# The MLP's first product by seven block products per pair of groups, with the sums of its weights held in place

## The chip, the cores and the metric

The kernel runs on one core of a Trainium2 chip. The metric is the time of one execution on the device in microseconds (us); the kernel before was run three times. A difference of about 0.2% (some 2 us) is what such a measurement can tell from none.

## What is computed

A decoder trunk of two layers on 512 tokens of 1024 features, all in 32-bit floats: a gated linear attention and an MLP, then a stick-breaking attention and an MLP, each followed by a layer norm. The change touches the MLPs, and to a small part the output product of the first attention:

```python
def sq_relu_mlp(x, w_up, w_down):
    h = jax.nn.relu(x @ w_up)       # (512, 1024) @ (1024, 4096)
    return (h * h) @ w_down         # (512, 4096) @ (4096, 1024)

h = layer_norm(DEEPNORM_ALPHA * h + sq_relu_mlp(h, mlp_w_up[layer], mlp_w_down[layer]),
               ln_g[layer, 1], ln_b[layer, 1])
```

## The kernel before

Every matrix is split into a high part that TensorE's fast 32-bit type holds exactly and a low part that is the rest: ScalarE (ACT) writes the high part (line 70 for weights, 98 for token matrices), VectorE (DVE) subtracts it from the whole (lines 72 and 99). A product is then three matmuls: high by high, high by low, low by high. Weights come from device memory in tiles of 128 partitions by 1024 (512 KB); their high and low parts live in pools of six tiles each (`split_tile`), so a split can run at most three pairs of tiles ahead of the product that uses it.

The MLP of a layer has eight groups of 512 of the 4096 inner features. `up(g)` makes one group of the squared first product: 96 matmuls of 512 columns, weights as the stationary side (lines 93 to 95), then relu on ACT (701) and a multiplication on DVE (703) into a tile `s2`. Only group 0 runs in halves of 256 columns. `down(g)` takes a pair of groups and adds its share of the second product to the rows `h`. It calls `seven`, which does the 2 by 2 blocks of that product by seven block products instead of eight, with sums of blocks of the tokens (lines 288, 360, 362, 374) and of the weights: 168 matmuls of 512 columns (line 346) in place of 192. In what follows the products of a `seven` are counted first to seventh in the order of the code. Each token block is split by `split_a` (lines 98 and 99).

Two of the four weight blocks are sums from the start: the tile is loaded by SyncE's queue (line 311) and a second block is added to it by an accumulating transfer that GpSimd (POOL) issues (line 305). The other two sums are made on DVE (lines 370 and 380), except in a call with `ends`, which adds blocks of device memory by more such transfers. The weight blocks live in eight tiles tagged B; a tile of the next call can be loaded only when its place is free.

The order of work in a layer's MLP:

```python
        sq = [up(0), up(1)]
        for h in hs:
            h.affine(vec, tc.keep_in_program_order)
        for g in range(0, NG - 2, 2):
            sq.append(up(g + 2))
            for _ in down(g):
                pass
            if g < NG - 4:
                sq.append(up(g + 3))
```

So an `up` lies ahead of each `down` whose group that `down` doesn't need yet, and the last `down` follows `up(7)` at once. The order of instructions on each engine is made by a scheduler when the program is built, unless a line says `keep_in_program_order`; on the chip each engine takes its queue in that order.

## Time and profile before

| | |
|---|---|
| median of three runs | 1120.47 us (1119.93 to 1120.68) |
| the profiled execution | 1120.0 us, of which the span from first to last instruction is 1118.1 us |
| TensorE clock granted | 0.999 of full |
| TensorE busy | 1110.2 us (99% of the span) |
| VectorE, ScalarE, GpSimd busy | 804.6, 551.2 and 166.2 us |
| transfers | 157.52 MB, 141 GB/s over the span |

Rows of a timeline give start and duration in us; a matmul's duration covers its way through the array, and the next one starts before it ends, so what a matmul costs in a stream is the distance between starts. "PEld" is the load of a matmul's stationary side.

### The profile page before, as it was taken

How to read it: one execution, taken by the hardware profiler on the slowest of the kernel's cores; microseconds unless marked ns; L12 is line 12 of the kernel's file. 1: busy time of each engine (PE TensorE's matmuls, PEld its weight loads, DVE VectorE, ACT ScalarE, POOL GpSimd, SP SyncE). 2: the span in 40 equal slices, each digit the busy share in tenths (PEclk: the TensorE clock that was granted, in tenths of full speed). 3: DMA queues.
4: the chain of work that ended last, by engine and by line, in shares of the span. 5: the costliest groups of instructions: out<-in, count | busy, mean ns of one | idle time of the engine just before them, and what ended most of it. 6: DMA issues, size and time to landing. Idle time of an engine off the chain costs nothing.

```text
span 1118.1 us, 14356 instructions
## 1 busy us (share of the span) xinstructions
PE 1110.2 (99%) x5519; PEld 920.1 (82%) x5519; DVE 804.6 (72%) x981; ACT 551.2 (49%) x829; POOL 166.2 (15%) x199
## 2 busy tenths in 40 slices
PE   9999999999999999999999999999999999999998
PEld 7888888898888888888888777778988888888886
DVE  4688649948956856858945888887489767667677
ACT  4455437643533534535634666664445435336363
POOL 1011222110100100122100434330200000000221
PEclk9999999999999999999999999999999999999999
DMA  8441399493670770887344121211946816706784
GB/s 250 120 132 57 112 261 221 132 256 113 189 207 24 200 208 19 204 199 143 113 114 132 57 76 39 76 38 56 276 122 191 245 52 164 231 19 186 178 131 89
DMA packets 105368, 157.52 MB, mean 141 GB/s; under 512 B 12306, under 2 KB 37266, under 8 KB 105300
## 3 DMA queue, kind: packets, MB, share of 16 engines
q1 hardware_dynamic: 87060, 120.96, 33.6%
q0 software_dynamic: 18240, 35.66, 18.6%
q8 instruction: 43, 0.70, 0.3%
q14 instruction: 25, 0.20, 0.1%
HBM read 153.45 MB, written 3.15 MB: 140 GB/s over the span
## 4 chain that ended last, share of the span: by engine, by line
PE 97%; DVE 2%; issue 0%; POOL 0%; POOLq 0%; DVEq 0%
PE ps L346 30%; PE ps L93 20%; PE ps L94 20%; PE ps L95 20%; PE ps L845 2%; PE ps L831 2%; PE ps L794 2%; PE ps L228 1%; PE ps L566 0%; DVE lo L72 0%; PE ps L121 0%; PE ps L631 0%; DVE bst L175 0%; PE ps L442 0%; PE ps L459 0%
## 5 line engine op out<-in xcount | busy, mean ns | idle before, releaser
L346 PE MATMUL ps<-hi,T 128*128 128x512 f32 x1008 | 313.2, 390 | 0.0
L93 PE MATMUL ps<-T,hi 128*128 128x512 f32 (+1 forms) x768 | 288.5, 376 | 0.0
L94 PE MATMUL ps<-T,hi 128*128 128x512 f32 (+1 forms) x768 | 285.5, 372 | 0.0
L95 PE MATMUL ps<-T,lo 128*128 128x512 f32 (+1 forms) x768 | 285.4, 372 | 0.0
L72 DVE TENSOR_TENSOR lo<-raw,hi 128x1024 fp32r<-128x1024 f32 x134 | 162.9, 1219 | 133.3 <-ACT hi L70 132.8
L70 ACT ACTIVATE hi<-raw 128x1024 fp32r<-128x1024 f32 x134 | 142.1, 1064 | 179.4 <-PE ps L94 61.3
L346 PEld LDWEIGHTS ps<-hi,T 128*128 128x128 f32 x1008 | 189.0, 188 | 40.0 <-DVE T L99 1.0
L346 PE MATMUL ps<-lo,T 128*128 128x512 f32 x504 | 196.1, 389 | 0.0
L70 ACT ACTIVATE hi<-B 128x1024 fp32r<-128x1024 f32 x108 | 114.1, 1059 | 160.4 <-PE ps L94 102.0
L72 DVE TENSOR_TENSOR lo<-B,hi 128x1024 fp32r<-128x1024 f32 x108 | 130.8, 1220 | 84.7 <-ACT hi L70 84.7
L95 PEld LDWEIGHTS ps<-T,lo 128*128 128x128 f32 x768 | 144.7, 188 | 25.1
L93 PEld LDWEIGHTS ps<-T,hi 128*128 128x128 f32 x768 | 144.7, 188 | 24.6 <-issue 0.9
L94 PEld LDWEIGHTS ps<-T,hi 128*128 128x128 f32 x768 | 144.8, 189 | 23.8 <-DVE T L99 0.2
L305 POOL DMA_DIRECT2D B<-in_mlp_w_down_dram x52 | 62.4, 1228 | 539.3 <-DMA B<-in_mlp_w_down_dram 424.7
L346 PEld LDWEIGHTS ps<-lo,T 128*128 128x128 f32 x504 | 94.6, 188 | 19.5
L93 PE MATMUL ps<-hi,T 128*128 128x512 f32 x256 | 102.4, 400 | 0.0
L95 PE MATMUL ps<-hi,T 128*128 128x512 f32 x256 | 100.1, 391 | 0.0
L94 PE MATMUL ps<-lo,T 128*128 128x512 f32 x256 | 100.0, 391 | 0.0
L168 DVE TENSOR_TENSOR h<-h,ps 128x512 f32<-128x512 f32 x110 | 74.7, 681 | 7.3 <-PE ps L95 4.2
L822 POOL TENSOR_TENSOR w<-w,r 128x512 f32<-128x512 f32 x32 | 53.0, 1658 | 131.6 <-DVE r L821 123.8
L821 DVE TENSOR_TENSOR_SCAN r<-r,begin 128x512 f32<-128x512 f32 x40 | 66.2, 1659 | 2.4 <-ACT r L818 2.2
L95 PEld LDWEIGHTS ps<-hi,T 128*128 128x128 f32 x256 | 48.1, 188 | 10.5 <-DVE T L99 0.2
(179 smaller groups left out, 1158.3 us busy)
## 6 DMA issues: line engine op xcount, KB each, us to landing
raw<-in_mlp_w_up_dram SPq DMA_DIRECT2D x64, 512.0 KB, 4.6
B<-in_mlp_w_down_dram SPq DMA_DIRECT2D x64, 512.0 KB, 6.0
B<-in_mlp_w_down_dram POOLq DMA_DIRECT2D x52, 512.0 KB, 7.9
raw<-in_gla_w_in_dram SPq DMA_DIRECT2D x20, 512.0 KB, 3.7
raw<-in_mlp_w_down_dram SPq DMA_DIRECT2D x16, 512.0 KB, 4.7
raw<-in_kv_w_dram SPq DMA_DIRECT2D x16, 512.0 KB, 4.2
B<-in_gla_w_o_dram POOLq DMA_DIRECT2D x14, 512.0 KB, 8.0
B<-in_gla_w_o_dram SPq DMA_DIRECT2D x8, 512.0 KB, 7.0
```

Of the source, the lines that this page charges most:

```text
L70: nc.scalar.activation(hi, raw, AF.Copy)
L72: nc.vector.tensor_tensor(lo, raw, hi.bitcast(F32), op=ALU.subtract)
L93: nc.tensor.matmul(ps, lhsT=a[0], rhs=b[0], start=first, stop=False)
L94: nc.tensor.matmul(ps, lhsT=a[0], rhs=b[1], start=False, stop=False)
L95: nc.tensor.matmul(ps, lhsT=a[1], rhs=b[0], start=False, stop=last)
L168: nc.vector.tensor_tensor(h, h, ps, op=op)
L305: nc.gpsimd.dma_start(out=b.rearrange("p (a b) -> p a b", a=2), in_=weights(k, h, j), accum_op=ALU.add)
L346: nc.tensor.matmul(banks[s], lhsT=a(k, s)[x], rhs=b[k][y], start=opens and (k, x, y) == (0, 0, 0), stop=closes and (k, x, y) == (3, 1, 0), ...
L794: nc.tensor.matmul(zs[b + a][:, at], lhsT=self.q[x][own, P * i:P * i + P], rhs=self.k[y][own, 0:n], start=(x + y == 0), stop=(x == 1), ski ...
L821: nc.vector.tensor_tensor_scan(down, down, begins[kind][:, ::-1], 1.0, op0=ALU.mult, op1=ALU.max)
L822: (nc.vector if kind == 2 else nc.gpsimd).tensor_tensor(w, w, r[:, 1:S + 1], op=ALU.mult)
L831: nc.tensor.transpose(out=ps[:, P * b:P * b + P], in_=w[:, P * b:P * b + P], identity=ident)
```

## The change

Groups 2 to 7 are no longer made by `up`, but in pairs by a new `up_seven(g, tokens)`: 2 by 2 blocks (two halves of the 1024 features, two halves of the 512 tokens, two groups), seven block products of 48 matmuls each. A moving side is a block of 256 tokens, so these matmuls are 256 columns wide and there are 336 to a pair, where two `up` had 192 of 512. The loop becomes: `down(g)`, then `up_seven(g + 2)`, whose two outputs the next `down` takes. No other product lies between them. The sums of token blocks are made once for a layer by `token_sums` after the first `down`, on DVE.

A new class `Blocks` loads the weight blocks for both kinds of call. It loads the two plain blocks first, then the two that are sums. The third and fourth sums (`third_sum`, `fourth_sum`) are now kept in program order on DVE behind the additions of results that stand before them in the code; with `ends` they are transfers from one B tile to another on the chip, not from device memory. Token sums in `seven` overwrite their inputs. The pools of high and low weight parts go from six tiles to five, the token tiles from eight to ten; the layer norm's vectors are loaded into tiles of other pools. In `up`, all even columns' squares go to ACT.

```diff
-        hi = wts.tile([P, 1024], F32R, tag="hi", bufs=6, name=nm("hi"))
+        hi = wts.tile([P, 1024], F32R, tag="hi", bufs=5, name=nm("hi"))
-    def ahead(a1, seventh=True):
-
-        s1, s2 = (lambda u: (u[:, :, 0:256], u[:, :, 256:512]))(unit(F32))
+    def ahead(a1):
+
         first = split_a(a1[:, :, 0:256])
-        nc.vector.tensor_tensor(s2, a1[:, :, 0:256], a1[:, :, 256:512], op=ALU.subtract)
-        return s1, s2, first, split_a(s2) if seventh else None
+        less = quarter()
+        nc.vector.tensor_tensor(less, a1[:, :, 0:256], a1[:, :, 256:512], op=ALU.subtract)
+        return first, lambda: split_a(less)
+    class Blocks:
+        def __init__(self, weights, pool):
+            self.weights, self.bs = weights, [[None] * 4 for _ in range(2)]
+            for i, k, j, other in ((2, 0, 0, None), (3, 1, 0, None), (1, 0, 1, (0, 0)), (0, 1, 1, (0, 1))):
+                for four_b, h in zip(self.bs, range(2)):
+                    b = pool.tile([P, 1024], F32, tag="B", bufs=8, name=nm("B"))
+                    nc.sync.dma_start(out=b.rearrange("p (a b) -> p a b", a=2), in_=weights(k, h, j))
+                    if other:
+                        self.more(b, h, *other)
+                    four_b[i] = b
+        def third_sum(self, ends):
+            for h, (b22, b12, b11, b21) in enumerate(self.bs):
+                if ends:
+                    nc.gpsimd.dma_start(out=b11, in_=b22, accum_op=ALU.add)
+                else:
+                    tc.keep_in_program_order(nc.vector.tensor_tensor(b11, b22, b11, op=ALU.add))
+        def fourth_sum(self, ends):
+            for h, (b22, b12, b11, b21) in enumerate(self.bs):
+                if ends:
+                    nc.gpsimd.dma_start(out=b21, in_=b11, accum_op=ALU.add)
+                else:
+                    tc.keep_in_program_order(nc.vector.tensor_tensor(b21, b21, b11, op=ALU.add))
...
-        tt(s1, a22, a21, op=ALU.subtract)
-        third = split_a(s1), split_b(1)
-        minus(s2, s1, a11)
+        seventh = seventh()
+        tt(a21, a22, a21, op=ALU.subtract)
+        third = split_a(a21), split_b(1)
+        minus(a11, a21, a11)
         product(*second, xs, True, True, 0, 0, last=True)
-        fourth = split_a(s2), split_b(2)
+        w.third_sum(ends)
+        fourth = split_a(a11), split_b(2)
         product(*third, zs, True, False, 1, 1)
-        minus(a12, a12, s2)
+        minus(a12, a12, a11)
         product(*fourth, ys, False, False, 0, 1)
+        w.fourth_sum(ends)
...
+        def up_seven(g, tokens):
+            w = Blocks(lambda k, h, j: block(mlp_w_up[l], 512 * k + 256 * h, 512 * (g + j)), mlp_)
...
+            def part(s, a, b, banks, opens, closes):
+                for f in (2 * s, 2 * s + 1):
+                    at = banks[s][:, 256 * (f % 2):256 * (f % 2) + 256]
+                    for k in range(4):
+                        for x, y in ((0, 0), (0, 1), (1, 0)):
+                            nc.tensor.matmul(at, lhsT=b[k][x][:, 128 * f:128 * f + 128], rhs=a(k)[y],
...
+            def close(s, banks, i, j, whole=False):
+                o = place(s, i, j)
+                if not whole:
+                    nc.vector.tensor_tensor(o, o, flat(banks[s]), op=ALU.add)
+                nc.scalar.activation(o, flat(banks[s]) if whole else o, AF.Relu, scale=-1.0 if j else 1.0)
+                nc.scalar.activation(o, o, AF.Square)
...
+            product(first, w.split(2), ys, True, False, keep, 0, 0)
+            product(second, w.split(3), xs, True, True, close, 0, 0)
+            w.third_sum(False)
+            product(third, w.split(1), zs, True, False, keep, 1, 1)
+            product(fourth, w.split(2), ys, False, False, keep, 0, 1)
+            product(third_, w.plain(1, 1), zs, False, True, close, 0, 1)
+            w.fourth_sum(False)
+            product(seventh, w.split(0), ys, False, False, close, 1, 1)
+            product(fourth_, w.split(3), ys, False, True, close, 1, 0, True)
+            return out
-        sq = [up(0), up(1)]
-        for h in hs:
-            h.affine(vec, tc.keep_in_program_order)
+        sq = [up(0), up(1, complete)]
         for g in range(0, NG - 2, 2):
-            sq.append(up(g + 2))
             for _ in down(g):
                 pass
-            if g < NG - 4:
-                sq.append(up(g + 3))
-        last, begun = up(NG - 1, lambda: ahead(sq[NG - 2]))
-        sq.append(last)
-        steps = down(NG - 2, begun=begun, norms=range(NT) if l == 0 else (2, 3), ends=True)
-        got = done(steps, work)
+            if g == 0:
+                tokens = token_sums()
+            sq = up_seven(g + 2, tokens)
+        steps = down(NG - 2, norms=range(NT) if l == 0 else (2, 3), ends=True)
+        got = done(steps, work, mlp_)
```

The scheduler's order moves in three places. First, on DVE before, layer 0, in the `up(3)` that runs ahead of `down(2)` (s_ is a group's tile, T_ a token tile, B_ a weight block, lo_ a low part; after "<-" stand the inputs):

```order
L703 TENSOR_TENSOR s_3040<-ps_2943,s_3040 128x512
L370 TENSOR_TENSOR B_3198<-B_3192,B_3198 128x1024
L362 TENSOR_TENSOR T_3202<-s_3040,s_2609 128x4x256
L99 TENSOR_TENSOR T_3246<-s_3040,T_3246 128x4x256
L360 SCALAR_TENSOR_TENSOR T_3202<-T_3202,s_2609 128x4x256
L72 TENSOR_TENSOR lo_3251<-B_3190,hi_3249 128x1024
L360 SCALAR_TENSOR_TENSOR s_3040<-s_3040,T_3202 128x4x256
L380 TENSOR_TENSOR B_3190<-B_3190,B_3188 128x1024
L72 TENSOR_TENSOR lo_3255<-B_3200,hi_3253 128x1024
L380 TENSOR_TENSOR B_3200<-B_3200,B_3198 128x1024
```

These are sums for `down(2)`: of its tokens (362, 360) and of its weights (370, 380). In the changed kernel the same sums of `down(4)` stand on DVE in the down itself. From its start (s_3574 and s_3575 are the two outputs of `up_seven(4)`; h_ rows are additions of finished products):

```order
L72 TENSOR_TENSOR lo_4091<-B_4018,hi_4089 128x1024
L290 TENSOR_TENSOR raw_4033<-s_3574 128x1024
L166 TENSOR_TENSOR h_1641<-h_1641,ps_4043 128x512
L385 TENSOR_TENSOR s_3574<-s_3575,s_3574 128x4x256
L166 TENSOR_TENSOR h_1642<-h_1642,ps_4057 128x512
L99 TENSOR_TENSOR T_4082<-raw_4033,T_4082 128x4x256
L99 TENSOR_TENSOR T_4086<-s_3574,T_4086 128x4x256
L72 TENSOR_TENSOR lo_4095<-B_4021,hi_4093 128x1024
L339 SCALAR_TENSOR_TENSOR s_3574<-s_3574 128x4x256
L166 TENSOR_TENSOR h_1641<-h_1641,ps_4098 128x512
L166 TENSOR_TENSOR h_1642<-h_1642,ps_4112 128x512
L316 TENSOR_TENSOR B_4010<-B_4024,B_4010 128x1024
```

and, six rows further, until the low part of the fifth product's tokens (T_4196):

```order
L166 TENSOR_TENSOR h_1644<-h_1644,ps_4153 128x512
L339 SCALAR_TENSOR_TENSOR s_3575<-s_3575,s_3574 128x4x256
L166 TENSOR_TENSOR h_1641<-h_1641,ps_4043 128x512
L72 TENSOR_TENSOR lo_4203<-raw_4199,hi_4201 128x1024
L166 TENSOR_TENSOR h_1642<-h_1642,ps_4057 128x512
L323 TENSOR_TENSOR B_4014<-B_4014,B_4010 128x1024
L323 TENSOR_TENSOR B_4016<-B_4016,B_4012 128x1024
L99 TENSOR_TENSOR T_4196<-s_3575,T_4196 128x4x256
```

The token and weight sums have moved from the `up` before into the `down`. Between these two fences stand the second third sum, T_4128, lo_4133, lo_4137 and the addition of ps_4139: from lo_4091 to T_4196 it is 25 rows.

Second, on DVE at the seam of the first `down` and the first `up_seven` of layer 0 (T_2776 is the room of the token sums, raw_2786 a part of one; the lo_ of B_2800 and B_2802 serve the first product, B_2811 the third):

```order
L164 SCALAR_TENSOR_TENSOR h_1644<-h_1644,ps_2525 128x512
L99 TENSOR_TENSOR T_2779<-T_2776,T_2779 128x4x256
L741 TENSOR_TENSOR T_2776<-T_2776,raw_2786 128x4x256
L72 TENSOR_TENSOR lo_2824<-B_2800,hi_2822 128x1024
L72 TENSOR_TENSOR lo_2828<-B_2802,hi_2826 128x1024
L99 TENSOR_TENSOR T_2777<-T_2776,T_2777 128x4x256
L72 TENSOR_TENSOR lo_2884<-B_2804,hi_2882 128x1024
L339 SCALAR_TENSOR_TENSOR T_2776<-T_2776,T_1653 128x4x256
L72 TENSOR_TENSOR lo_2888<-B_2806,hi_2886 128x1024
L748 TENSOR_TENSOR T_2776<-T_2776,T_1654 128x4x256
L72 TENSOR_TENSOR lo_2950<-B_2808,hi_2948 128x1024
L339 SCALAR_TENSOR_TENSOR T_2776<-T_2776,T_1655 128x4x256
```

Before, no row of this kind stood there: the splits of an `up` followed the additions of a `down` directly. Four rows further down (a split, a sum and an addition among them) stands lo_2954 of B_2811.

Third, on SyncE's queue, the loads of `down(4)` in the changed kernel, with the loads of `up_seven(4)` ahead of them and of `up_seven(6)` behind:

```order
L301 DMA B_3568<-in_mlp_w_up_dram 128x2x512
L301 DMA B_3571<-in_mlp_w_up_dram 128x2x512
L301 DMA B_4010<-in_mlp_w_down_dram 128x2x512
L301 DMA B_4012<-in_mlp_w_down_dram 128x2x512
L301 DMA B_4014<-in_mlp_w_down_dram 128x2x512
L301 DMA B_4016<-in_mlp_w_down_dram 128x2x512
L301 DMA B_4018<-in_mlp_w_down_dram 128x2x512
L301 DMA B_4021<-in_mlp_w_down_dram 128x2x512
L301 DMA B_4024<-in_mlp_w_down_dram 128x2x512
L301 DMA B_4027<-in_mlp_w_down_dram 128x2x512
L64 DMA raw_4199<-in_mlp_w_down_dram 128x2x512
```

and before, the loads of `down(2)`, between them those of an `up` (raw_):

```order
L311 DMA B_3182<-in_mlp_w_down_dram 128x2x512
L311 DMA B_3185<-in_mlp_w_down_dram 128x2x512
L311 DMA B_3188<-in_mlp_w_down_dram 128x2x512
L311 DMA B_3190<-in_mlp_w_down_dram 128x2x512
L64 DMA raw_2922<-in_mlp_w_up_dram 128x2x512
L64 DMA raw_2928<-in_mlp_w_up_dram 128x2x512
L311 DMA B_3192<-in_mlp_w_down_dram 128x2x512
```

The eight B tiles now pass from one call straight to the next: B_4018 and B_4021 take the place of the two tiles that the fourth sum of `up_seven(4)` reads last.

More of the change, by code (lines that the diff above doesn't have):

```diff
@@ L300, in seven @@
         a11, a21, a12, a22 = a1[:, :, lo_t], a1[:, :, hi_t], a2[:, :, lo_t], a2[:, :, hi_t]
[L301 to L329 removed]
+        w = Blocks(weights, pool)
+        split_b, plain_b = w.split, w.plain
         seen = set()
@@ L353, in product @@
                 add(s, banks, i, j, last)
-        s1, s2, first, seventh = begun or ahead(a1)
+        first, seventh = begun or ahead(a1)
         product(first, split_b(2), ys, True, False, 0, 0)
@@ L654, in yoco_kernel @@
     gate(1, 1, pcs)
-    begun = ahead(onT[0], seventh=False)
+    begun = ahead(onT[0])
     turn_gated(0, 1)
@@ new lines, in up_seven, with place, flat, keep @@
+        def up_seven(g, tokens):
+            w = Blocks(lambda k, h, j: block(mlp_w_up[l], 512 * k + 256 * h, 512 * (g + j)), mlp_)
+            first, second, third, fourth, third_, seventh, fourth_ = tokens
+            out = [four(), four()]
+            ys, xs, zs = ([None, None] for _ in range(3))
+            def part(s, a, b, banks, opens, closes):
+                if opens:
+                    banks[s] = bank()
+                for f in (2 * s, 2 * s + 1):
[3 more added lines that the diff above has]
+                            nc.tensor.matmul(at, lhsT=b[k][x][:, 128 * f:128 * f + 128], rhs=a(k)[y],
+                                             start=opens and (f % 2, k, x, y) == (0, 0, 0, 0),
+                                             stop=closes and (f % 2, k, x, y) == (1, 3, 1, 0),
+                                             skip_group_check=True)
+            def place(s, i, j):
+                return out[j][:, 2 * s:2 * s + 2, 256 * i:256 * i + 256]
+            def flat(ps):
+                return ps.rearrange("p (a b) -> p a b", a=2)
+            def keep(s, banks, i, j):
+                nc.scalar.activation(place(s, i, j), flat(banks[s]), AF.Copy)
+            def close(s, banks, i, j, whole=False):
[4 more added lines that the diff above has]
+                nc.scalar.activation(o, o, AF.Square)
+            def product(a, b, banks, opens, closes, then, *args):
+                for s in range(2):
+                    part(s, a, b, banks, opens, closes)
+                    then(s, banks, *args)
+            product(first, w.split(2), ys, True, False, keep, 0, 0)
[8 more added lines that the diff above has]
+            return out
@@ L857, in yoco_kernel @@
     parts = [(oA.hi[0][:, i, :], oA.lo[0][:, i, :]) for i in range(4)]
-    vec, vcols = lnvec(0, 1), lncols(1, 0)
+    vec = lnvec(0, 1, *(sbp.tile([P, D], F32, name=n) for n in ("lng", "lnb")))
+    vcols = lncols(1, 0)
     pairs[0].keys()
@@ L886, in yoco_kernel @@
     h3T = Split()
-    vec = lnvec(1, 0)
     def part2(t):
@@ L925, in done1 @@
         late = []
+        vec = None
         for t in steps:
+            if not vec:
+                vec = lnvec(1, 1, *(pool.tile([P, D], F32, tag="B", bufs=8, name=nm("B")) for _ in range(2)))
             if t < 0:
```

123 lines of the change are left out of this document (67 added, 56 removed).

## The prediction

> **What bounds the kernel now.** I read the shares of the engines first, then the chain that ended last.
>
> ```profile
> PE 1110.2 (99%) x5519; PEld 920.1 (82%) x5519; DVE 804.6 (72%) x981; ACT 551.2 (49%) x829; POOL 166.2 (15%) x199
> PE 97%; DVE 2%; issue 0%; POOL 0%; POOLq 0%; DVEq 0%
> ```
>
> The chain follows TensorE (PE) for 97% of the span, and PE is busy for 99%: every matmul taken away is worth its time, as long as the other engines still keep up. So the question is what DVE, the next busiest, has to do in each stage. That is read from busy times by stretch, here for `up(3)` of layer 0 and the `down(2)` behind it (columns: stretch, its length, then busy time and count of PE, PEld, DVE, ACT, POOL; granted clock, share of the DMA engines, GB/s).
>
> ```profile
> 321.00:364.50 43.50, 43.50 (x194) 36.03 (x193) 27.85 (x28) 15.52 (x20) 0.00 (x0) 1.00 0.23 74
> 364.50:402.60 38.10, 38.10 (x170) 31.56 (x169) 28.91 (x32) 18.36 (x19) 4.77 (x4) 1.00 0.81 219
> ```
>
> PE has no gap in either. DVE is busy 28 to 29 us in each: the work is spread evenly, with 15.6 us free in the `up` and 9.2 in the `down`. Third, the distance of matmuls in a timeline of PE, 512 columns wide in a `seven` and 256 wide in the halves of `up(0)`; the second piece is the first and the last of 76 matmuls in a row.
>
> ```profile
> 190.05 0.61 PE L346 MATMUL ps<-hi,T 128*128 128x512 f32 x2
> 190.50 0.39 PE L346 MATMUL ps<-lo,T 128*128 128x512 f32 x1
> 190.73 0.61 PE L346 MATMUL ps<-hi,T 128*128 128x512 f32 x2
> ...
> 226.33 0.28 PE L93 MATMUL ps<-T,hi 128*128 128x256 f32 x1
> ...
> 235.33 0.28 PE L93 MATMUL ps<-T,hi 128*128 128x256 f32 x1
> ```
>
> Three matmuls of 512 take 0.68, so 0.2267 each; 75 of 256 take 9.00, so 0.120 each, 1.06 times one half.
>
> **The change part by part.** *What it removes.* Two `up` are 192 x 0.2267 = 43.5 us, as the first stretch above is long. An `up_seven` is 336 x 0.120 = 40.3. There are three pairs in each of two layers: 6 x 3.2 = 19.2 us less of PE's work.
>
> The 256-wide price includes a weight load for each matmul:
>
> ```profile
> L93 PEld LDWEIGHTS ps<-T,hi 128*128 128x128 f32 x768 | 144.7, 188 | 24.6 <-issue 0.9
> ```
>
> A load lasts 188 ns, longer than the 120 between the narrow matmuls, so loads overlap one another. [...]
>
> *What it moves: DVE's work.* Before, an `up` lies ahead of each `down`, and in it DVE makes the sums that the `down` needs. This is that place in `up(3)`:
>
> ```profile
> 344.89 0.68 DVE L703 TENSOR_TENSOR s<-ps,s 128x512 f32<-128x512 f32 x1
> 345.49 1.22 DVE L370 TENSOR_TENSOR B<-B,B 128x1024 f32<-128x1024 f32 x1
> 346.62 1.22 DVE L362 TENSOR_TENSOR T<-s,s 128x1024 f32<-128x1024 f32 x1
> 347.76 1.22 DVE L99 TENSOR_TENSOR T<-s,T 128x1024 fp32r<-128x1024 f32 x1
> 348.89 1.22 DVE L360 SCALAR_TENSOR_TENSOR T<-T,s 128x1024 f32<-128x1024 f32 x1
> ```
>
> In a row, an operation of 1024 columns costs 1.137 us and one of 512 costs 0.60 (345.49 - 344.89), though each is shown 0.08 longer. [...]
>
> After the change the `down` follows an `up_seven` whose last product makes a quarter of its tokens. The sums of tokens that take in that quarter, and the weight sums, held behind the additions, can't run ahead: ten operations (362, 360 twice, the third token split, 370 and 380 twice each, the new difference and its split), 11.4 us, move into the `down`: 28.9 + 11.4 = 40.3 against 38.1 of PE. In the `up_seven` DVE has 14 weight splits and 4 sums, and 6 additions: 18 x 1.137 + 6 x 0.60 = 24.1 of 40.3. So DVE has too little time in one stage and much in the other, and the deadlines inside the `down` decide.
>
> *The steady downs* (`down(2)`, `down(4)`, four in all). The nearest case in the trace is the last `down` of layer 1, which already follows its second `up` directly. Its start on PE, and DVE's row from the first weight split to the low part of the fifth product's tokens:
>
> ```profile
> 1070.85 0.39 PE L346 MATMUL ps<-hi,T 128*128 128x512 f32 x1
> ...
> 1071.93 1.23 DVE L72 TENSOR_TENSOR lo<-B,hi 128x1024 fp32r<-128x1024 f32 x1 [2.28 <-ACT hi L70]
> 1073.08 0.68 DVE L703 TENSOR_TENSOR s<-ps,s 128x512 f32<-128x512 f32 x1
> ...
> 1084.12 1.22 DVE L360 SCALAR_TENSOR_TENSOR s<-s,T 128x1024 f32<-128x1024 f32 x1
> 1085.26 0.68 DVE L168 TENSOR_TENSOR h<-h,ps 128x512 f32<-128x512 f32 x1
> 1085.85 1.22 DVE L72 TENSOR_TENSOR lo<-raw,hi 128x1024 fp32r<-128x1024 f32 x1
> 1086.99 1.22 DVE L99 TENSOR_TENSOR T<-s,T 128x1024 fp32r<-128x1024 f32 x1
> ```
>
> The split begins 1.08 into the `down`, and the low part is there at 1088.21, 17.36 into it, after 11 wide and 6 narrow operations without a pause. PE needs it behind four products and 6 more matmuls: 102 x 0.2267 = 23.1. So 5.8 us were spare. The changed order has 25 rows between the same ends, 17 wide and 8 narrow (the second order fence): 17.36 + 6 x 1.137 + 2 x 0.60 = 25.4, which is 2.3 late even if it starts as early.
>
> It starts later. Its first row, the split of B_4018, needs a tile whose place is free only when the fourth sum of the `up_seven` has been made, and which is loaded and then added to by POOL's transfer. These are such a load and the POOL issue behind it in the trace of the queues, POOL's group on the page, the spread of all its landings, and ACT's high part:
>
> ```profile
> 361.37 0.37 SPq L311 DMA_DIRECT2D B<-in_mlp_w_down_dram  x1
> 365.46 1.19 POOL L305 DMA_DIRECT2D B<-in_mlp_w_down_dram  x1 [56.54 <-DMA B<-in_mlp_w_down_dram]
> ...
> B<-in_mlp_w_down_dram POOLq DMA_DIRECT2D x4, 512.0 KB, 8.4
> ...
> DMA to landing us min/median/max: 5.7/7.9/13.8
> ...
> L70 ACT ACTIVATE hi<-B 128x1024 fp32r<-128x1024 f32 x108 | 114.1, 1059 | 160.4 <-PE ps L94 102.0
> ```
>
> From the start of an `up_seven`: the fifth product ends after 240 x 0.12 = 28.8 us; its addition takes DVE to 29.7; the first half of the fourth sum ends at 30.9; 4.1 to POOL's issue, 35.0; 8.4 to landing, 43.4; 1.06 for the high part, 44.5. The `up_seven` is 40.3 long, so the split starts 4.2 into the `down` in place of 1.08: 25.4 + 3.1 = 28.5, against 23.1. PE stands 5.4 us, four times: 21.6. With the shortest landing, 5.7, the split starts near 1.7, and the stall is 2.9; with the longest, 13.8, it is 10.8. I take the 8.4 of this same stage.
>
> *The first downs of the layers* (two). Their weights are there early, behind `up(0)` and `up(1)`; the path has 6 wide and 3 narrow operations more than the model: 26.0 - 23.1 = 2.9 each, 5.8.
>
> *The first `up_seven` of each layer* (two). `token_sums` puts 14 wide operations (15.9 us) between the first `down` and its end. By the order at that seam, the low part lo_2824 stands behind an addition that follows the last matmul (0.3 + 0.6), the split of T_2779 and the sum 741: 4.5 after the start with its own time. PE has 9 matmuls, 1.1 us, ahead of its need: 3.4 of stall. lo_2954 comes 11 wide and one narrow operation later, at 17.7; matmul 106 wants it at 3.4 + 12.7 = 16.1: 1.6 more. Both layers: 10.0. A gain is excluded here, since no such operation stood there before. Nothing shows at best, if the splits went ahead of the sums; at worst all 15.9 do, 31.8 in place of 10.0, which takes the sum to 1162.
>
> *The last downs* (two). Their weight sums are transfers, so DVE has only two wide and three narrow operations more than the model, one narrow in layer 1, and the late start: 17.36 + 2.3 + 1.8 + 3.1 = 24.5 and 23.3, so 1.4 + 0.3 = 1.7.
>
> *Edits taken at nothing.* Pools of five: a split can run 2.5 products ahead in place of three, and a product is at least 5.8 us long; were that cover gone, each of the 1.22 us splits at a seam would show, about 1 us each. The additional ACT work:
>
> ```profile
> L701 ACT ACTIVATE s<-ps 128x512 f32<-128x512 f32 x64 | 38.0, 594 | 25.4 <-PE ps L95 24.8
> B<-in_gla_w_o_dram POOLq DMA_DIRECT2D x14, 512.0 KB, 8.0
> ```
>
> An `up_seven` has 22 activations of 0.59, 13.0 us, so ACT in the two stages goes from 33.9 (the two stretches) to at most 46.9 of 78.4: half of its time stays free. In the attention's product 8 transfers in place of 14 go through POOL, which is idle 85% of the span; were that cover gone, one late landing would cost the 8.0 of the row.
>
> *The sum.* The profiled execution took 1120.0 us, 0.47 under the median. Less 19.2 of matmuls, plus stalls of 21.6 + 5.8 + 10.0 + 1.7 = 39.1: 1139.9, forecast 1140. With the ends of the landing (2.9 and 10.8 in the four downs) it is 1130 to 1162.
>
> **The rivals.** *PE stays the bound: faster.* If the splits of a `down` are made early enough (the low part by 24.3 into it, so 1.2 late or less: with 6 x 1.2 and 10.0 the stalls stay 2 us below the 19.2), and only the seam of the first `up_seven` shows, the time is 1120.0 - 19.2 + 10.0 = 1110.8. For it: DVE has 16 us free in an `up_seven`, the landing can take 5.7, and 5.8 were spare in the model. Against it: 2.3 late by counting alone, and the sums can't be made before the last product that they read. Chance 0.20.
>
> *Half of it:* part of the path overlaps, stalls of about 1.5 to 3 us in a `down`: 6 x 2.2 + 10 = 23, less 19.2, about 1124, between 1118 and 1129. It lies around no change. Chance 0.10, of which 0.07 within the 0.2% (2 us, what a measurement of this kernel can tell) and 0.03 slower.
>
> *Transfers come late: much slower.* At the DMA share of 0.81 of a `down`, the accumulating transfers take the longest landing everywhere: 1162; more, if the third product's tiles, which are the first ones loaded for the next call, are late too. For it: every B tile now passes directly to the next call. Against it: the shares of the DMA engines in an `up` are 0.23. Chance 0.12.
>
> *Narrow matmuls wait for their loads: 188 ns each.* 336 x 0.188 = 63.2 in place of 43.5, 6 x 19.7 = 118 more: 1238. The 76 narrow matmuls at 0.120 speak against it. [...]
>
> **How the numbers follow.** The forecast case has 0.57 (1130 to 1162 for itself). Faster: 0.20; within 0.2%: 0.07; slower: 0.57 + 0.03 + 0.12 + 0.01 = 0.73. The range from 1110 to 1162 leaves out half of the faster case (0.10), half of the late transfers (0.06) and the narrow matmuls (0.01).
>
> **What the new profile would show.** Right: matmuls of an `up_seven` 0.12 apart; DVE without a gap in the first 28 us of a `down`, and PE's gap there of 3 to 6 us ahead of its fifth product, ended by the token split, line 99; the first weight split of a steady `down` waiting for a transfer; two gaps of PE at the start of a layer's first `up_seven`, ended by a weight split, line 72. Wrong: no gap of PE in the downs (then the sums ran ahead, and it is faster by 10); gaps ended by a transfer ahead of other products (then DVE's path wasn't the limit); or a PE that is 99% busy with matmuls further apart than 0.12.

## The result, and the profile after

The changed kernel takes 1197.43 us (median of four, 1195.18 to 1199.74) against 1120.58: a ratio of 1.0685, with an interval from 1.0671 to 1.0698. It is slower, as forecast, but by 77 us and not by 20: outside the range. The profiled execution took 1198.84 us, its span is 1196.9, which is 78.8 over the span before.

On the page after, PE is no longer busy throughout, and the chain of waits passes through DVE and transfers:

```profile
PE 1126.7 (94%) x6383; PEld 963.1 (80%) x6383; DVE 897.4 (75%) x1057; ACT 635.3 (53%) x957; POOL 170.5 (14%) x205
PE 71%; DVE 17%; DMA 7%; ACT 3%; issue 2%; POOL 0%; POOLq 0%; DVEq 0%; ACTq 0%
```

PE has 864 matmuls more, as the change says (6 x 144). It is busy 1126.7 us, where 1110.2 less the 19.2 saved would be 1091.0: 35.7 us too many, though no matmul was added beyond those counted. The rest of the loss is standing time. These are PE's waits by what ended them (us in total, times, longest):

```profile
PE ps L370 <- ACT T L98: 25.9, 6, 11.4
PE ps L370 <- DVE T L99: 20.8, 11, 2.8
PE ps L773 <- ACT T L98: 7.0, 2, 3.5
PE ps L370 <- DVE lo L72: 4.5, 4, 1.6
...
PE ps L370 <- ACT hi L70: 0.8, 2, 0.4
...
PE ps L773 <- DVE lo L72: 0.6, 2, 0.3
```

Together 59.6 us. So the 78.8 are: -19.2 for matmuls, +59.6 of standing, +35.7 of PE's own time, and 2.7 elsewhere. Busy times by stretch, for down(2), up_seven(4), down(4) of layer 0 and the last down of layer 1, show where (columns as in the prediction):

```profile
352.10:398.90 46.80, 41.00 (x170) 32.09 (x169) 39.06 (x40) 21.00 (x22) 5.01 (x5) 0.96 0.78 202
398.90:440.10 41.20, 41.15 (x340) 40.82 (x339) 27.89 (x27) 26.67 (x37) 4.52 (x4) 1.00 0.50 131
440.10:487.50 47.40, 42.11 (x168) 33.12 (x167) 39.06 (x40) 20.77 (x22) 5.28 (x5) 0.93 0.76 198
1135.00:1187.00 52.00, 40.59 (x171) 32.53 (x170) 36.35 (x45) 23.80 (x28) 8.57 (x10) 0.90 0.55 124
```

The `up_seven` is as long as forecast (41.2 with three or four matmuls of the next `down` among its own) and has no gap. Before, a `down` took 38.1; now 47, and in it PE's own 168 matmuls take 41 to 42 us at a mean granted clock of 0.96 and 0.93. That is the second loss. In PE's timeline of down(4) one sees how it begins:

```profile
451.92 0.50 PE L370 MATMUL ps<-hi,T 128*128 128x512 f32 x1 [1.10 <-ACT T L98]
...
453.37 0.73 PE L370 MATMUL ps<-hi,T 128*128 128x512 f32 x2 [0.72 <-DVE T L99]
...
461.38 0.50 PE L370 MATMUL ps<-lo,T 128*128 128x512 f32 x1 [0.66 <-DVE lo L72]
...
470.89 0.96 PE L370 MATMUL ps<-hi,T 128*128 128x512 f32 x2 [2.82 <-DVE T L99]
471.65 0.63 PE L370 MATMUL ps<-lo,T 128*128 128x512 f32 x1
472.08 1.48 PE L370 MATMUL ps<-hi,T 128*128 128x512 f32 x3
473.36 0.63 PE L370 MATMUL ps<-lo,T 128*128 128x512 f32 x1
```

Two short gaps stand at the start of the third product, one at that of the fourth, and one of 2.82 in the first matmuls of the fifth, which the token split of line 99 ends. The matmuls behind it last 0.63 us in place of 0.39, and from 472.08 to 473.36 three of them take 1.28, 0.427 each in place of 0.2267, until about 474.6. This is the granted clock at half: the trace has it at 0.50 from 471.21 to 474.62. It has thirteen such stretches ahead of the last 3 us of the execution, all behind gaps. A view of just these thirteen ends with this sum (their length, then the busy time of each engine in them):

```profile
sum 68.28, PE 51.87 PEld 41.90 DVE 53.38 ACT 15.20 POOL 5.33; mean PE 3.99 PEld 3.22 DVE 4.11 ACT 1.17 POOL 0.41
```

By the two distances of wide matmuls, 0.427 and 0.2267, PE loses 51.87 x (1 - 0.2267 / 0.427), an estimate of 24 us. So about two thirds of the 35.7 are the lower clock; the other 11 or so were not taken apart.

DVE and ACT in the same down, whose first matmul is at 439.98:

```profile
444.99 1.23 DVE L72 TENSOR_TENSOR lo<-B,hi 128x1024 fp32r<-128x1024 f32 x1 [3.25 <-ACT hi L70]
...
469.61 1.22 DVE L99 TENSOR_TENSOR T<-s,T 128x1024 fp32r<-128x1024 f32 x1
```

```profile
443.89 1.06 ACT L70 ACTIVATE hi<-B 128x1024 fp32r<-128x1024 f32 x1 [2.93 <-DMA B<-in_mlp_w_down_dram]
444.86 0.61 ACT L792 ACTIVATE s<-s 128x512 f32<-128x512 f32 x1
448.91 1.07 ACT L70 ACTIVATE hi<-B 128x1024 fp32r<-128x1024 f32 x1 [3.44 <-DMA B<-in_mlp_w_down_dram]
449.88 1.04 ACT L98 ACTIVATE T<-raw 128x1024 fp32r<-128x1024 f32 x1
450.83 1.04 ACT L98 ACTIVATE T<-s 128x1024 fp32r<-128x1024 f32 x1
```

The row of DVE that the prediction starts with, the split of the third product's first weight tile, begins 5.0 us into the `down` (forecast: 4.2), behind a transfer. What the prediction had not seen stands on ACT: the third product's second tile lands at 448.9, and two token splits of line 98 are queued behind it. The second of them, at 450.83, is the one that PE waits for; DVE had finished its data at 449.1. The last downs have the same in large. ACT, POOL and PE in the last down of layer 1:

```profile
1143.06 1.06 ACT L70 ACTIVATE hi<-B 128x1024 fp32r<-128x1024 f32 x1 [4.81 <-DMA B<-in_mlp_w_down_dram]
1144.03 1.04 ACT L98 ACTIVATE T<-raw 128x1024 fp32r<-128x1024 f32 x1
1155.20 1.06 ACT L70 ACTIVATE hi<-B 128x1024 fp32r<-128x1024 f32 x1 [10.13 <-DMA B<-B]
1156.16 1.04 ACT L98 ACTIVATE T<-s 128x1024 fp32r<-128x1024 f32 x1
```

```profile
1140.35 1.20 POOL L308 DMA_DIRECT2D B<-in_mlp_w_down_dram  x1 [4.87 <-DVE raw L290]
1147.67 0.90 POOL L314 DMA_DIRECT2D B<-B  x1 [6.11 <-DVE lo L72]
1151.59 0.86 POOL L314 DMA_DIRECT2D B<-B  x1 [3.02 <-DMA B<-in_mlp_w_down_dram]
```

```profile
1157.26 0.79 PE L370 MATMUL ps<-hi,T 128*128 128x512 f32 x1 [11.37 <-ACT T L98]
```

The third weight sum is a transfer from tile to tile here. The block that it adds is an accumulating load, issued at 1134.27, ahead of the `down`, which lands 12.8 us later, at 1147.1. The transfer starts at 1147.67, just behind that and behind a low part on DVE that ends at the same time, and ACT waits for it until 1155.20: 7.5 us. No product ahead of the fourth needs this sum. But the tokens of the third (line 98 at 1156.16), whose data DVE had finished by 1141.9, stand behind it in ACT's order, and PE waits for these 11.4 us.

### The profile page after: what moved, and what is told of

The parts are those of the page before. It is cut to its first block, busy times and chain, and to the rows that moved or that the text cites. A ratio compares the mean times of both kernels' runs of the same rounds, so it can differ in the third digit from the quotient of the medians.

```text
span 1196.9 us, 16386 instructions
## 1 busy us (share of the span) xinstructions
PE 1126.7 (94%) x6383; PEld 963.1 (80%) x6383; DVE 897.4 (75%) x1057; ACT 635.3 (53%) x957; POOL 170.5 (14%) x205
## 4 chain that ended last, share of the span: by engine, by line
PE 71%; DVE 17%; DMA 7%; ACT 3%; issue 2%; POOL 0%; POOLq 0%; DVEq 0%; ACTq 0%
PE ps L370 18%; PE ps L773 12%; PE ps L93 11%; PE ps L94 11%; PE ps L95 11%; DMA B<-in_mlp_w_down_dram 6%; DVE lo L72 5%; DVE T L99 4%; DVE B L323 2%; DVE h L166 2%; PE ps L949 2%; PE ps L935 1%; PE ps L898 1%; DMA B<-B 1%; ACT hi L70 1%
## 5 line engine op out<-in xcount | busy, mean ns | idle before, releaser
L70 ACT ACTIVATE hi<-B 128x1024 fp32r<-128x1024 f32 x180 | 189.8, 1056 | 197.7 <-PE ps L370 91.2
L370 PEld LDWEIGHTS ps<-hi,T 128*128 128x128 f32 x1008 | 197.3, 197 | 99.2 <-ACT T L98 28.6
L72 DVE TENSOR_TENSOR lo<-B,hi 128x1024 fp32r<-128x1024 f32 x180 | 216.4, 1224 | 64.5 <-ACT hi L70 63.1
L773 PE MATMUL ps<-T,hi 128*128 128x256 f32 x1344 | 246.3, 286 | 7.0 <-ACT T L98 7.0
L773 PE MATMUL ps<-T,lo 128*128 128x256 f32 x672 | 190.0, 287 | 0.8 <-DVE lo L72 0.6
L72 DVE TENSOR_TENSOR lo<-raw,hi 128x1024 fp32r<-128x1024 f32 x98 | 119.1, 1221 | 64.2 <-ACT hi L70 61.9
L93 PE MATMUL ps<-T,hi 128*128 128x512 f32 (+1 forms) x384 | 139.0, 363 | 0.7 <-ACT T L98 0.7
L94 PE MATMUL ps<-T,hi 128*128 128x512 f32 (+1 forms) x384 | 136.2, 355 | 0.0
L95 PE MATMUL ps<-T,lo 128*128 128x512 f32 (+1 forms) x384 | 136.0, 354 | 0.0
L773 PEld LDWEIGHTS ps<-T,lo 128*128 128x128 f32 x672 | 129.7, 195 | 2.1 <-DVE lo L72 2.0
L99 DVE TENSOR_TENSOR T<-s,T 128x1024 fp32r<-128x1024 f32 (+1 forms) x58 | 65.5, 1129 | 26.9 <-ACT T L98 26.9
L95 PEld LDWEIGHTS ps<-T,lo 128*128 128x128 f32 x384 | 72.6, 189 | 10.1
## 6 DMA issues: line engine op xcount, KB each, us to landing
B<-in_mlp_w_down_dram POOLq DMA_DIRECT2D x32, 512.0 KB, 11.3
```

Of the source, the lines that this page charges most:

```text
L70: nc.scalar.activation(hi, raw, AF.Copy)
L72: nc.vector.tensor_tensor(lo, raw, hi.bitcast(F32), op=ALU.subtract)
L93: nc.tensor.matmul(ps, lhsT=a[0], rhs=b[0], start=first, stop=False)
L94: nc.tensor.matmul(ps, lhsT=a[0], rhs=b[1], start=False, stop=False)
L95: nc.tensor.matmul(ps, lhsT=a[1], rhs=b[0], start=False, stop=last)
L99: keep(nc.vector.tensor_tensor(lo, ps, hi.bitcast(F32), op=ALU.subtract))
```

## The experiments

Each is the changed kernel (1197.4 us) with the edit shown. Times are medians of four or more; ratios are to the kernel before. Executions of one such kernel lie 2 to 12 us apart (those of the kernel before 1 to 3), so a difference of a few us between two of them is weak evidence by itself.

**One row of DVE: the fourth sum behind the fifth product's token split.**

```diff
-        w.fourth_sum(ends)
-        p3, p7 = (split_a(a12), plain_b(1, 1)), (seventh, split_b(0))
+        p3 = split_a(a12), plain_b(1, 1)
+        w.fourth_sum(ends)
+        p7 = seventh, split_b(0)
```

> The changed kernel with one edit: in a down, the fourth weight sum (two wide DVE operations) is written behind the token split of the fifth product in place of ahead of it. Theory A (DVE's row is what ends PE's gap of 2.8 us ahead of the fifth product in six downs, and PE's clock is granted lower for some microseconds after such a gap): the token split comes 2 x 1.137 = 2.3 us earlier, the six gaps fall from 2.8 to about 0.6, the slow matmuls behind them (about 1.6 us each) mostly go as well: 1197 less 6 x (2.2 + 1.6) = about 1174. Theory B (the split waits for ACT or a transfer, and the row on DVE only looks full): the gaps stay at 2.8 and the time within 2 us of 1197.

1195.0 us (1.066, 1.0644 to 1.0675). The six gaps did shrink, to 0.54 or 0.55; one of them, with DVE's row ahead of it:

```profile
467.81 1.22 DVE L99 TENSOR_TENSOR T<-s,T 128x1024 fp32r<-128x1024 f32 x1
```

```profile
469.08 0.73 PE L369 MATMUL ps<-hi,T 128*128 128x512 f32 x2 [0.54 <-DVE T L99]
469.65 0.40 PE L369 MATMUL ps<-lo,T 128*128 128x512 f32 x1
```

and behind a gap of 0.54 the matmuls are fast (0.40). But the time hardly changed: the scheduler also rebuilt the seam of the first `up_seven`, where PE's waits in the two layers together rose from 7.6 us to about 19:

```profile
PE ps L773 <- ACT hi L70: 10.2, 8, 3.0
PE ps L773 <- DVE lo L72: 8.5, 4, 3.0
```

(six of the eight are 0.7 each, one in every `up_seven`). Theory A's cause is right for its gap; as a forecast of the whole time (1174) it failed.

**The last downs' sums on DVE.**

```diff
-        steps = down(NG - 2, norms=range(NT) if l == 0 else (2, 3), ends=True)
+        steps = down(NG - 2, norms=range(NT) if l == 0 else (2, 3))
```

> The changed kernel with the third and fourth weight sums of the last down of each layer made on DVE, as in the other downs, in place of transfers from tile to tile. Theory A (the two gaps of 11.2 and 11.4 us are due to these transfers: ACT's high part of the summed tile waits for one, and the token split of the third product stands behind it on ACT): the 11 us gaps fall to the pattern of the steady downs (about 0.9 + 0.7 ahead of the third product, 2.8 ahead of the fifth), so 2 x (11.3 - 5) = about 13 less: 1184. Theory B (the gap comes from the accumulating load that lands late, which stays): the gaps stay over 9 us, and the four wide operations on DVE make it a little slower: 1197 to 1203.

1193.5 us (1.0645, 1.0619 to 1.0672). The 11 us gaps are gone; each last down now has the steady pattern with four gaps, 5.5 and 6.7 us in all:

```profile
PE ps L370 <- DVE T L99: 27.8, 15, 2.8
```

So A is right about the gaps. The gain is 4 us in the medians, a third of the 13 forecast; between the two profiled executions it is 10.8, and executions of this kernel lie up to 7.5 us apart.

**Filler on PE.** 40 matmuls of 512 columns ahead of the last downs' third product; its bank is opened afresh behind them, so nothing of them is left.

```diff
+        if warm:
+            zs[0] = bank()
+            for _ in range(warm):
+                tc.keep_in_program_order(nc.tensor.matmul(zs[0], lhsT=second[0](0, 0)[0], rhs=second[1][0][0],
+                                                          start=True, stop=True, skip_group_check=True))
         product(*third, zs, True, False, 1, 1)
```

> The changed kernel with 40 additional matmuls of 512 columns (9.1 us of work whose result is overwritten) in the last down of each layer, right where PE stands for 11 us ahead of the third product. Theory A (the clock is granted lower because PE stood): the matmuls behind the gap are 0.23 us apart from the first on in place of 0.43, the mean clock of the two last downs rises from 0.86 and 0.90 to over 0.95, and the kernel is 3 to 6 us faster though it does more. Theory B (the matmuls behind the gap are slow for another reason, their weight loads or the transfers beside them): they stay 0.43 apart and the time stays within 1 us or grows.

1202.1 us (1.0721, 1.0694 to 1.0748): slower by 5. The stretch of 8 us behind the gap in layer 0, of the changed kernel and then with filler (PE busy and count, clock behind POOL's column):

```profile
549.00:557.00 8.00, 6.38 (x15) 4.63 (x16) 6.44 (x8) 4.54 (x5) 1.65 (x2) 0.53 0.71 139
```

```profile
549.60:557.60 8.00, 7.11 (x29) 5.27 (x30) 7.93 (x9) 2.16 (x3) 0.85 (x1) 1.00 0.64 126
```

With PE kept busy the clock is 1.00 in place of 0.53, and 29 matmuls start in 8 us where 15 did: here the clock fell because PE stood. In layer 1 the wait outlasted the filler by 4.0 us. In layer 0 the time was lost to DVE's row, which the scheduler had ordered otherwise (gaps of 2.1 and 2.4 us that additions and a layer norm end). So A's cause is right and its forecast of 3 to 6 us less is not, and what the slow clock costs in all isn't settled by this run.

**Two plain ups in place of each up_seven**, at the same place in the loop, without token sums.

```diff
-            if g == 0:
-                tokens = token_sums()
-            sq = up_seven(g + 2, tokens)
+            sq = [up(g + 2), up(g + 3)]
```

> The changed kernel with its new product undone at the same place of the loop: two plain ups in place of each up_seven, no token sums; the order down, two ups, down and the other edits stay. PE has 19 us more to do. Theory A (the stalls come from a down that follows its second group of tokens directly, with all its sums on DVE in the down): the downs keep gaps ahead of the fifth product, about 2.3 us each with 1.6 of low clock behind, and the last downs something like it; only the late first weight tile goes, since B tiles are free during two ups: 1120 + about 30 = 1150, 1140 to 1160. Theory B (the block products themselves bring the stalls, by their use of B tiles and of DVE): the gaps go, and the time is that of the kernel before, 1118 to 1125.

1150.8 us (1.0268, 1.025 to 1.0286). Theory A; that it is right to the microsecond is luck, since its gaps were to be 2.3 us, and the last downs were to have them as well:

```profile
PE ps L372 <- DVE T L99: 17.9, 7, 2.8
```

```profile
437.46:478.85 41.39, 38.58 (x169) 31.35 (x168) 38.24 (x40) 19.77 (x21) 4.79 (x4) 1.00 0.51 156
844.60:887.60 43.00, 40.19 (x169) 32.48 (x168) 38.42 (x40) 19.76 (x21) 4.82 (x4) 0.96 0.53 155
```

The new order of the loop, with the change's other edits left in (pools, sums kept in program order), costs 30 us with no block product in the ups. The last downs have no gap here. The two rows differ only in the clock behind the same gap of 2.81 us: 1.00 and 0.96, which is 1.6 us.

**A fixed place for each weight block.**

```diff
-                    b = pool.tile([P, 1024], F32, tag="B", bufs=8, name=nm("B"))
+                    b = pool.tile([P, 1024], F32, tag=f"B{2 * i + h}", bufs=1, name=nm("B"))
```

> The changed kernel with a fixed place for each of the eight weight blocks of a call (eight tags of one tile in place of one tag of eight): the sum that the third product needs takes the place of the same block of the call before, which is free after that call's third product, and no longer that of a tile that its fourth sum reads last. DVE's and ACT's orders stay. Theory A (late tiles are the other half of the stalls): the gaps ahead of the third product of the four steady downs (about 3.5 us together, and slow matmuls behind) go, the gaps of 2.8 ahead of the fifth stay; the second sums of the last downs land early, so their transfers no longer make PE stand 11 us. By the downs of the two-ups kernel, which has these tiles early (41.4 to 43.0 us each, and a last down without a gap): about 1145 to 1160. Theory B (the transfers land 11 us late wherever they start, or the order on ACT decides): 1185 to 1197.

1168.8 us (1.0427, 1.0387 to 1.0466), between the two theories: 28.7 less, by tiles that come earlier. The 11 us gaps are gone with the transfers still there, and the steady downs take 42 to 44 us. Two things remain, the fifth product's gap, and a new one, since a fixed place can also come free late:

```profile
PE ps L370 <- DVE T L99: 18.4, 8, 2.8
PE ps L370 <- ACT hi L70: 10.9, 6, 2.4
```

**Fixed places, and the last downs' sums on DVE** (both edits above).

> Fixed places for the weight blocks, and the last downs' third and fourth sums on DVE. Theory A (with early tiles the transfers of the last downs hide, so sums on DVE only bring their gap of 2.8 ahead of the fifth product there too): 4 to 8 us slower than the kernel with fixed places alone. Theory B (transfers from tile to tile are late by themselves): 5 to 15 us faster than that kernel.

1177.1 us (1.0514, 1.0471 to 1.0556), 8.4 more than with transfers: A. In these two pairs of runs the transfers hurt where what they add lands late, and not where it is early.

**The loop turned**, each `up_seven` one down ahead; the fourth output tile is paid for with pools of four weight parts.

```diff
-        for g in range(0, NG - 2, 2):
-            for _ in down(g):
-                pass
-            if g == 0:
-                tokens = token_sums()
-            sq = up_seven(g + 2, tokens)
+        tokens = token_sums()
+        after = up_seven(2, tokens)
+        for g in range(0, NG - 2, 2):
+            for _ in down(g):
+                pass
+            sq, after = after, up_seven(g + 4, tokens) if g < 4 else None
```

> The changed kernel with the loop turned: each up_seven runs one down ahead (up_seven(2) before down(0), and so on), so that the tokens of a down are there one stage early; a fourth output tile is paid for with pools of four high and four low weight parts. Theory A (the gap ahead of the fifth product comes from the token sums, which can't be made before the last product of the up_seven): the six gaps of 2.8 us and the two seams of 3.5 behind the token sums go, the late weight tiles stay (third product, and most of the 11 us of the last downs): about 1155, 1145 to 1175. Theory B (the late tiles and the shorter pools decide, the token sums only fill waiting time): 1185 or more.

1132.0 us (1.0098, 1.0083 to 1.0114): 65 us less, more than A had it, since the late tiles that A left in place no longer made PE stand either. The first `up_seven` of layer 0, `down(0)` and `up_seven(4)`:

```profile
270.30:318.80 48.50, 43.54 (x338) 42.93 (x336) 43.31 (x42) 34.67 (x47) 3.25 (x3) 0.93 0.40 124
318.80:357.50 38.70, 38.70 (x175) 31.95 (x174) 35.04 (x37) 22.00 (x23) 5.08 (x5) 1.00 0.72 186
357.50:397.30 39.80, 39.80 (x333) 39.80 (x332) 31.44 (x31) 26.09 (x35) 4.16 (x4) 1.00 0.69 186
```

PE has no gap and a full clock in the last two; DVE has 35.0 and 31.4 where it had 39.1 and 27.9. Most of what is left is in the first row, and 4.6 us in the attention.

**Turned loop, fixed places, sums on DVE.**

> The turned loop, fixed places and the last downs' sums on DVE together (pools of four). Theory A (late token sums and late weight tiles are all that makes PE stand): PE is bound by its own work again: 1120 - 19 = 1101, with a few waits left 1101 to 1112, faster than the kernel before. Theory B (DVE's sum of work, or pools of four, becomes the bound): 1120 or more.

1143.8 us (1.0199, 1.0178 to 1.0219). Theory A failed. The downs wait here for high parts (6.4 us in six waits, up to 2.0, where the turned loop had 0.8). The run holds two edits at once; that this wait is the fixed places' own is likely, since they had it above, and not shown apart.

**The turned loop paid for with nine token tiles in place of ten.**

> The turned loop (each up_seven one down ahead), the fourth output tile paid for with nine token tiles in place of ten; high and low weight parts stay at five. Theory A (pools of four cost the other turned kernel its 4.6 us gap in the attention and part of the late splits): 5 to 12 us faster than that kernel's 1132: 1120 to 1127. Theory B (with nine tiles the splits of tokens wait for room): 1140 or more, with gaps of PE ended by token splits.

1163.7 us (1.0372, 1.0342 to 1.0402): B. One token tile less cost more than the larger pools of weight parts gave, by 31.7 us. Three further kernels wrote the token sums ahead of the second `up`. Since the last token split overwrites tokens that this `up` reads, it takes changed tokens in them, and waits for the sums: their results are wrong, and only their times can be read.

> As the turned loop with nine token tiles, and the token sums written ahead of the second up, so that DVE can make them during the two ups. Theory A (the 4.4 us and 1.3 us gaps at the first up_seven of each layer are the 14 token sums ahead of its weight splits on DVE): these gaps fall under 1 us and the kernel is 4 to 8 us faster than without that edit, below the kernel before if that one is at 1124 or less. Theory B (they are late weight splits by short pools): no change.

> The same early token sums with ten token tiles and pools of four weight parts. Theory A (the short pools cost time in the attention and in the last downs): 5 to 12 us slower than with nine token tiles and pools of five. Theory B (nine token tiles cost as much): within 3 us of it.

> Early token sums, nine token tiles, and the last downs' third and fourth sums on DVE in place of transfers. Theory A (in the turned loop the tokens are early, so what is left of waiting in the last two downs, 4 to 6 us a layer, is the transfers' lateness): 4 to 8 us faster than with transfers. Theory B (DVE's row is full there): same or slower.

1161.6, 1151.4 and 1156.4 us, with 19 to 24 us of waits for token splits in the `up`: they tell the cost of that wait and decide none of the theories. (The second was to be slower than the first and is 10 us faster.)

**The token sums early, but for the last split**, which stays behind the second `up` (turned loop, pools of four; then with two raw tiles and five low parts; then with the last downs' sums on DVE).

```diff
-            put(h0[:, :, hi_t], l0[:, :, hi_t], s2)
+            rest = lambda: put(h0[:, :, hi_t], l0[:, :, hi_t], s2)
...
+        sq = [up(0)]
+        tokens, rest = token_sums()
+        sq.append(up(1, complete))
+        rest()
+        after = up_seven(2, tokens)
```

> The turned loop with pools of four weight parts, and the token sums, all but the last token split (it overwrites tokens that the second up still reads), written ahead of the second up. Theory A (what the turned loop still loses at the first up_seven of each layer, 4.4 and 1.3 us of gaps with slow matmuls behind, is the token sums standing among its weight splits on DVE): the gaps fall under 1 us and the kernel takes 1132 - 8 = 1124, 1118 to 1127. Theory B (the gaps come from weight splits that are late for want of room in pools of four): 1130 to 1134.

> As the kernel before it in this list, with the room for the fourth output tile taken otherwise: four high parts, five low parts, two tiles of raw weights in place of three. Theory A (raw weights are loaded early enough with two, and the 4.6 us gap in the attention comes from pools of four low parts): 3 to 6 us faster. Theory B (plain weights in the ups and the attention need three tiles of raw): 10 us slower or more.

> The turned loop with pools of four and early token sums, and the last downs' sums on DVE in place of transfers. Theory A (the waits left in the last two downs, 1.8 + 0.8 + 0.8 us in layer 1 and 0.8 in layer 0, are those for summed tiles that come by transfer): 2 to 5 us faster than with transfers. Theory B (DVE is full there): 0 to 5 us slower.

1127.7 us (1.006, 1.0045 to 1.0075), 1140.5 (1.0172, 1.0155 to 1.0188) and 1121.9 (1.0012, 0.9992 to 1.0032). The first: 4 us less than the turned loop, half of what A had, with one gap of 2.1 us left where A had none over 1; the second: B; the third: A, 5.8 less, which is the time of the kernel before. In this third kernel, `up_seven(2)`, `down(0)` and `up_seven(4)` of layer 1, and the first row of its page:

```profile
838.10:878.65 40.55, 40.55 (x338) 40.36 (x336) 33.08 (x33) 27.58 (x38) 2.40 (x3) 1.00 0.45 142
878.65:917.39 38.74, 38.74 (x175) 31.94 (x173) 35.04 (x37) 22.11 (x23) 6.48 (x6) 1.00 0.74 191
917.39:957.20 39.81, 39.81 (x333) 39.81 (x332) 31.46 (x31) 26.08 (x35) 3.51 (x4) 1.00 0.67 188
```

```profile
PE 1101.1 (98%) x6383; PEld 949.7 (85%) x6383; DVE 903.3 (80%) x1065; ACT 637.2 (57%) x957; POOL 162.6 (14%) x197
```

The same 6383 matmuls take 1101.1 us of PE in place of 1126.7. In layer 1 PE takes 274.6 us from the start of the first `up_seven` (838.10) to the end of the last `down` (1112.65); before, six `up` and four downs took 283.1 (826.05 to 1109.11): 8.5 less, and the forecast was 9.6 a layer. So the gain of the block products is real, and it is used up ahead of layer 1: the attention's output product starts 10.4 us later than before (182.72 against 172.36), and in layer 0 the first `up_seven`, with a gap of 2.9 in it, takes 46.0 us where the one above takes 40.6.

**The pools back at five for the attention**, four from the first MLP on.

> The turned loop with early token sums and the last downs' sums on DVE, and pools of weight parts in two sizes: five of each up to the first MLP, four from there on. Theory A (what keeps the turned kernel at the time of the kernel before, 1122, is the gap of 5.6 us in the attention and the slow matmuls behind it, from pools of four there): 6 to 9 us faster, 1113 to 1116, so faster than the kernel before. Theory B (that gap has another cause, or the loss is in the MLPs): 1120 to 1123.

1120.4 us (0.9999, 0.9991 to 1.0008). The time is B's, though A was right about the cause of the gap: the 5.6 us in the attention are gone, and gaps of 3.3, 2.5 and 1.7 stand in the first two `up` behind the exchange of the pools. Two more, of 2.2 in the first `up_seven` and 3.3 in a `down` of layer 0, remain.

## Why the prediction was wrong

The forecast was 57 us too low. Two steps failed. The last downs were priced at 1.7 us of standing and had 22.5: 20.8 more. And the sum took PE's price of a matmul as unchanged behind a stall, where PE's own time came out 35.7 us longer. Together these are 56.5.

| step of the prediction | forecast | measured |
|---|---|---|
| matmuls saved | -19.2 | `up_seven` 40 to 41 us, as forecast; 8.5 us in layer 1 of the kernel with the least waits |
| steady downs, four | 21.6 | gaps of 5.8, 5.3, 5.0 and 6.6: 22.8 |
| first downs, two | 5.8 | 3.9 + 2.8 = 6.7 |
| first `up_seven`, two | 10.0 | 3.8 + 3.8 = 7.6 |
| last downs, two | 1.7 | 11.2 + 11.4 = 22.5 |
| PE's own time behind gaps | not in the sum | 35.7, of it about 24 by the clock |

*The steady downs.* The cause was right: tokens and weight sums that can't run ahead, on a DVE row too long for the `down`, behind a first tile that comes late (5.0 into the down against 4.2). The kernel with two plain ups shows the first half of it alone, the fixed places the second, the turned loop takes away both. That the size fits is partly luck. In down(4) the low part of the fifth product's tokens is there 30.9 us into the down, where 28.5 was forecast; but PE comes to it at 28.1 and not at 23.1, 2.5 of that for earlier gaps and most of the rest for the clock, so that the gaps add up to 5.3. Their place was only half right: 2.8 us stand ahead of the fifth product. The rest stands ahead of the third, where ACT holds a token split behind a high part whose transfer has not landed, and ahead of the fourth, whose weight sum and its split come late on DVE. The prediction had counted DVE's queue and taken ACT's work at nothing, because half of ACT's time was to stay free (by its own 46.9 of 78.4 it is 40%); a free share says nothing of the order in the queue.

*The first `up_seven`.* The first gap is 3.5 where 3.4 was forecast. The profile puts it down to a token split on ACT; the weight split that the prediction named ends at the same time (309.12 and 1.22 on DVE, PE starts at 310.35), so this run can't tell them apart. The second gap is 0.3 and not 1.6.

*The last downs.* The step that failed is "Their weight sums are transfers, so DVE has only two wide and three narrow operations more". It priced what the transfers take off DVE and not when they land. The block that they add is itself an accumulating load that lands 12 us into the `down`, the transfer waits for it, and the high part of the sum stands ahead of the third product's tokens on ACT. Taking the transfers away ended it, and so did having the tiles earlier, with the transfers still there. ACT's order is the third condition; no run changed it alone.

*The clock.* The prediction took a stall to cost its length. PE's busy time came out 35.7 us over the sum; the stretches at half clock account for about 24 of it, the filler shows for one gap that the clock fell because PE stood (1.00 in place of 0.53 with PE kept busy), and in the kernel with the least waits (the same matmuls, 25.6 less) it goes with the gaps. In the `down` shown the matmuls at half clock came 0.427 apart in place of 0.2267; nine of the thirteen stretches lasted 3.41 us, two 6.83, and the two at the gaps of 11 us 10.24 and 13.65. A gap of 2.8 us had such a stretch behind it in all six cases of the changed kernel, and in four of six with two plain ups. The kernel before shows nothing of it, since it has no such gap in its MLPs: the sum had no row to price it by, and should have named it as a cost left out.

*The rivals.* "Transfers come late" had a chance of 0.12 and 1162. It came nearest: accumulating loads of the down weights landed after 11.3 us in the median, where 8.4 had been taken. But it priced them in the steady downs, and they cost most in the last downs and through ACT, with the clock on top. The narrow matmuls did not wait for their loads: they are 0.12 apart in the `up_seven` shown, as the rows of before had it, with loads of 195 ns in the mean. A small slip: by the prediction's own working the shortest landing gives a stall of 2.7 and not 2.9, which moves the lower end by under 1 us.

## What to carry to other kernels

When a change lets a stage depend on the product right ahead of it, list every in-order queue that prepares that stage, ACT's as well as DVE's, and price each row by when its last input lands: in the last `down` of layer 1 one late transfer held a token split on ACT from 1141.9, when its data was there, to 1156.16, and PE for 11.4 us. A stall of TensorE cost more than its length here, because the clock was at half behind most gaps of 2.8 us and more: gaps of 59.6 us cost about 24 more by the clock, by the estimate above. Turning the loop by one stage was worth 65 us here, but the room for it had to come from other pools, and the gaps that this opened elsewhere took back what the block products gave.

## What the hardware showed that was not expected

The granted clock behind a gap of the same length was not always the same: with one gap of 2.81 us a `down` took 41.4 us in one layer and 43.0 in the other. The clock's record in the traces shows what went with it. In the changed kernel all thirteen stretches at half clock are 3.41 us long or two to four times that, and they start a whole number of 3.41 us apart. In the kernel with two plain ups, where the six gaps are equal, the clock fell behind four, each with more than 1.9 us of its idle time inside one step of that grid (1.94, 2.05, 2.81 and 2.81), and stayed full behind two that a step's border cuts into 1.83 + 0.98 and 1.89 + 0.92. The stretches behind one of either kind (as in the prediction's table, clock behind POOL's column):

```profile
462.78:466.20 3.42, 2.44 (x11) 2.02 (x12) 3.42 (x4) 0.00 (x0) 0.00 (x0) 1.00 0.89 290
872.38:875.80 3.42, 3.42 (x9) 2.65 (x8) 3.42 (x4) 0.00 (x0) 0.00 (x0) 0.50 0.89 305
```

No limit can be read from these: in the changed kernel two gaps of 0.86 and 0.72 us, 1.58 together in one step, had a stretch at half clock behind them once. The time also varied: ten executions of the third kernel with early token sums go from 1118.4 us at a mean clock of 0.997 to 1130.1 at 0.991. The matmuls behind single gaps of 0.54 and 0.66 us stayed at 0.39 to 0.40 us.

A tile-to-tile accumulating transfer of 512 KB took 7.4 us from issue to landing in the last `down` shown, and 5.9 in the median of the twelve. Accumulating loads of the down weights landed after 11.3 us in the median, where 7.9 was the median before:

```profile
B<-in_mlp_w_down_dram POOLq DMA_DIRECT2D x32, 512.0 KB, 11.3
```
